# Sparse attention on one core: the compression's first layer in split products, and the query projections spread over more steps

## The chip, the cores and the metric

The kernel runs on one core of a Trainium2 chip. The metric is the device time of one execution in microseconds (us). The core has a matrix engine (PE, with its weight loads shown as PEld), three other compute engines (DVE, ACT, POOL) and a queue that starts transfers (SP). Each engine takes its instructions in the order of the program and waits on semaphores of the others.

## What is computed

The reference is a two-layer decoder trunk on 512 tokens of width 1024: four feed-forward half steps, a gated linear attention with pooling, and, in the second layer, a sparse attention of three branches. The change lies in the sparse attention. Cut to that:

```python
def nsa(h, w_in, cmp_pe, cmpk_w1, cmpk_w2, cmpv_w1, cmpv_w2, w_out):
    q, kc, vc, ks, vs, kw, vw, gates = jnp.split(h @ w_in, cuts, axis=-1)
    ...
    cidx = np.arange(ncmp)[:, None] * 16 + np.arange(32)[None]     # 31 windows of 32 tokens
    def compress(z, w1, w2):
        zb = z[:, cidx] + cmp_pe[None, None, :, None, :]
        zb = zb.transpose(0, 1, 3, 2, 4).reshape(B, ncmp, G, 32 * 64)
        return jax.nn.gelu(zb @ w1) @ w2                           # 2048 -> 256 -> 64
    k_cmp, v_cmp = compress(kc, cmpk_w1, cmpk_w2), compress(vc, cmpv_w1, cmpv_w2)
    # per block of queries: softmax over k_cmp, over the selected keys ks, over the window kw;
    # the three results are gated, added, and projected by w_out
```

There are 16 query heads in 2 key groups, so zb has 62 rows (31 windows by 2 groups) for the keys and 62 for the values.

## The kernel before

**Splitting.** Almost every product is made of float32 values that are split into a high part (float32r, written by ACT) and a low part (the rest, written by DVE or POOL), and takes three one-pass products: hi by hi, lo by hi, hi by lo (`mm3`, L342 to L344). A weight comes by DMA as a raw tile `wr` of 128 x 1024, then `half_hi` (L206, ACT) and `half_lo` (L218, DVE; in the attention loop L216, POOL) write `wh` and `wl` in two halves of 512 columns. The first layer of the compression is the exception: its weights (units "w1", eight of them, four for keys and four for values) are not split, and `hidden` (L1356) multiplies plain float32 tiles, `Z` by `wr`.

**The stream of weights.** `W.next` hands out the next unit. `W.pump(n)` issues loads and conversions for units up to n ahead (n is 2 where nothing is said), at the place in the program where it stands. There are three raw tiles and three pairs `wh`, `wl`; a load waits until the raw tile three units earlier is done with, a conversion until the products with the pair three conversions earlier are done.

**The order at the start of the sparse attention** (`mixer1`; PE, DVE and ACT follow it as written):

1. project kc; finish the norm; pump (splits the unit ks)
2. project vc; get `rstd`; `relay("k")` (L1300, 4 DVE operations), `windows("k")` (L1307, 2 DVE operations that make Z); `negb`; pump (unit w1 of keys, part 0: nothing to split); `relay("v")`, `windows("v")`
3. `keys(0)`: project ks; pump(3) (reaches w1 part 1 and kw); `kf`, `k2`, four ACT copies `kA`, two DVE operations `kB`
4. `hidden(0, "k", 0)`: parts 0 and 1, each followed by a pump
5. `keys(1)`: project kw, then as in 3
6. `hidden(0, "k", 2)`: parts 2 and 3
7. project query block 0 (unit qq0); pump; `gelu(0)` (L1363 to L1370); `qevac(0, ...)` (L1239, L1246, L1250, L1254)
8. `hidden(1, "v", 0)`, whose first pump splits the unit vsw 0; `values` part 0 with it; `hidden(1, "v", 2)`; `values` parts 1 and 2, and `values_out` (L1272 to L1278)

**The attention loop** goes over steps t; head pair m has twelve steps, in each of which scores (L1467), row maxima, exponentials, transposes (L1514), splits of the transposed weights (L1525, L1534) and products with values (L1546, L1548) of different heads stand beside each other. `QP` says in which of the twelve steps how many of the 24 products (`qproj`, L1232) of the next head pair's query projection are issued, `QEV` in which steps the parts of its evacuation (`qevac`) stand, and `FILL` puts the splits of finished outputs (`osplit`) and early products of the output projection (`oproj`) into the last steps. The query projection has one bank of PSUM, tile X.

Of the kernel before, what the change touches and what calls it, by code (L numbers as in the profile page):

```python
# [6 lines left out]
F32 = mybir.dt.float32  # L7
F32R = mybir.dt.float32r
BF = mybir.dt.bfloat16
U32 = mybir.dt.uint32  # L10
AF = mybir.ActivationFunctionType
# [18 lines left out]
def half_step():  # L30

    ev = [(t, 2 * q + e) for q in range(PLAIN) for t in "gu" for e in range(2)]
    m0, end = 2 * PLAIN, len(PARTS) - 1
    d = [("d", p, i, 0, PARTS[p]) for p in range(end) for i in DORD]
    for m in range(m0, 22):
        x, y = (d.pop(0) if d and m > m0 else None for _ in range(2))
        if m == m0:
            ev += [(n, m) for n in (1, 2, 5, 6)]  # L40
        else:
            ev += [e for e in ((1, m), (2, m), (7, m - 1), (5, m), x, (6, m), (3, m - 1), (4, m - 1), y) if e]
    ev += [(7, 21), (4, 21), (3, 21)] + [("d", end, i, 0, 4) for i in DORD[:2]]
    return ev + [("d", end, i, 4 * (n < 2), PARTS[end]) for n, i in enumerate(DORD)]


def unit_shapes():
    out = []

    def ffn(j):  # L50
        for e in half_step():
            if e[0] in ("g", "u"):
                out.append(((e[0], j, e[1]), 1024, True))
            elif e[0] == 1:
                q, t = divmod(e[1], 2)
                for f in (2 * q, 2 * q + 1):
                    out.append((("gu"[t], j, f), 1024, True))
            elif e[0] == "d" and e[3] == 0:
                out.append((("d", j, e[1], e[2]), PARTS[e[1]] * 128, True))

    ffn(0)
    out.append((("gr",), 128, True))
    for nm in ("k0", "k1", "q0", "q1"):
        out.append(((nm,), 1024, True))
    for i in range(4):
        out.append((("v", i), 1024, True))
    for i in (3, 2, 1, 0):
        out.append((("p", i), 1024, True))
    for i in range(4):
        out.append((("gg", i), 1024, True))  # L70
    for d in range(KB):
        out.append((("ao", d), 1024, True))
    ffn(1)
    ffn(2)
    for nm in ("kc", "vc"):
        out.append(((nm,), 1024, True))
    out.append((("ks",), 1024, True))
    for nx in (("w1", 0, 0), ("w1", 0, 1), ("kw",), ("w1", 0, 2), ("w1", 0, 3), ("qq", 0), ("w1", 1, 0), ("w1", 1, 1),
               ("vsw", 0), ("w1", 1, 2), ("w1", 1, 3), ("vsw", 1), ("vsw", 2)):
        n = 304 * (VPART[nx[1] + 1] - VPART[nx[1]]) if nx[0] == "vsw" else 1024  # L80
        out.append((nx, n, nx[0] != "w1"))
    for m in range(1, KB):
        out.append((("qq", m), 1024, True))
    for d in range(KB):
        out.append((("co", d), 1024, True))
    ffn(3)
    return out
# [9 lines left out]
def _build(ctx, tc, nc, a, stages):  # L97
# [10 lines left out]
    V, S, P, TE = nc.vector, nc.scalar, nc.gpsimd, nc.tensor  # L108
    f32 = lambda ap: ap.bitcast(F32)
# [3 lines left out]
    for k in range(KB):  # L113
        t = res.tile([128, T], F32, name=f"h{k}")
# [7 lines left out]
    zero = cst.tile([128, 64], F32, name="zero")  # L122
# [6 lines left out]


    units = [u for u in unit_shapes()]

    def used(key):
# [104 lines left out]
    W = Stream()  # L238
# [945 lines left out]
    def mixer1(nm, nxt):  # L1184
        with ExitStack() as c:
# [24 lines left out]
            o = [op_.tile([128, T], F32, name=f"o{m}") for m in range(KB)]  # L1210
# [70 lines left out]
            with ExitStack() as c2:  # L1281
                s2 = c2.enter_context(pool("m1t", 1, reuse_waits="tile"))
# [3 lines left out]
                R, Z = {}, {}  # L1286
# [4 lines left out]
                def pn():  # L1291
                    return ps.tile([128, T], F32, name="pn", bufs=2)
# [8 lines left out]
                    R[nmx] = r  # L1301

                def windows(nmx):
                    z = s2.tile([128, 1024], F32, name="Z" + nmx)[:, 0:992].rearrange(
                        "p (a b c) -> p a b c", a=16, b=2)
                    for s in range(2):
                        V.tensor_add(z[:, 8 * s:8 * s + 8],  # L1307
                                     R[nmx][:, :, s:s + 31, :].rearrange("p g n r -> p r g n"),
                                     vec[:, C_PE + 8 * s:C_PE + 8 * s + 8][:, :, None, None]
                                     .to_broadcast([128, 8, 2, 31]))  # L1310
                    Z[nmx] = z

                pn0 = pn()
                pkc = pj()
# [8 lines left out]
                V.tensor_scalar(rhalf, rcol, 0.5, None, op0=OP.mult)  # L1323
                relay("k", pkc)
                windows("k")
                V.tensor_copy(negb, neg)
                W.pump()
                relay("v", pvc)
                windows("v")

                def keys(br, key):
# [16 lines left out]
                def hidden(wi, nmx, i0):  # L1348
                    if i0 == 0:
                        hbank[wi] = pn()  # L1350
                    ph = hbank[wi]
                    for i in range(i0, i0 + 2):
                        _, _, raw = W.next("w1", wi, i)
                        for q in range(4):
                            kt = 4 * i + q
                            TE.matmul(ph[0:62, 0:256], Z[nmx][:, kt].rearrange("p a b -> p (a b)"),  # L1356
                                      raw[:, q * 256:(q + 1) * 256], start=kt == 0, stop=kt == 15)
                        W.pump()

                def gelu(wi):  # L1360
                    ph = hbank[wi]
                    x = s2.tile([62, 256], F32, name="gx", bufs=2)
                    V.tensor_copy(x, ph[0:62, 0:256])  # L1363
                    u = aq.tile([62, 256], F32, name="gu", bufs=2)
                    V.tensor_mul(u, x, x)
                    V.tensor_scalar(u, u, 0.044715, 1.0, op0=OP.mult, op1=OP.add)
                    V.tensor_mul(u, u, x)
                    S.activation(u, u, AF.Tanh, scale=0.7978845608028654)
                    V.tensor_scalar(u, u, 1.0, 0.5, op0=OP.add, op1=OP.mult)
                    V.tensor_mul(u, u, x)  # L1370
                    hid.append(u)

                keys(0, "ks")
                hidden(0, "k", 0)
                keys(1, "kw")
                qload(0)
                hidden(0, "k", 2)
                bank = pj()
                for k in range(KB):
# [224 lines left out]
            NU = len(U)  # L1604
            W.pool_lo = True
            at_t = lambda t: (U[t // 3], t % 3) if 0 <= t < 3 * NU else None
            QEV = ({8: 0, 9: 1, 10: 2, 12: 3, 14: 4, 16: 6, 19: 5}, {11: 0, 12: 1, 13: 2, 14: 3, 16: 4, 17: 6, 18: 5})
            QP = {}
            for m, k, ws in ((1, 3, (3, 3, 2, 3, 4, 1, 4, 4)), (2, 0, (3, 3, 3, 4, 3, 3, 3, 2)),
                             (3, -2, (2, 2, 3, 2, 4, 2, 3, 2, 2, 2))):  # L1610
                QP[m] = {k + i: (sum(ws[:i]), sum(ws[:i + 1])) for i in range(len(ws))}
            CMP = ({5: 0, 6: 1, 8: 2, 11: 3, 12: 4}, {5: 0, 6: 1, 9: 2, 10: 3, 12: 4})
            CMPW = {1: (-2, 0), 3: (0, 1), 5: (1, 3)}
# [15 lines left out]

            begun = {0: 7, 1: 5}  # L1630
            FILL = {}
            for m, t in enumerate((84, 84, 87, 89, 90, 92, 97)):
                where = (xp, ("xh", 8), ("xl", 8)) if m < 4 else (aq, ("qA", 3), ("qB", 4))
                FILL.setdefault(t, []).append((osplit, m, P if m < 6 else V, *where))
            for n, t in enumerate((93, 95, 98, 98)):
                FILL.setdefault(t, []).append((W.half, n % 2 * 512))
            for n, t in enumerate((88, 90, 90, 94, 94, 96, 98, 103, 104, 104, 104, 106)):
                d, k = divmod(n, begun[0])
                FILL.setdefault(t, []).append((oproj, d, k, k + 1))
            for t in range(-3, 3 * NU + 11):  # L1640
# [14 lines left out]
                if at_t(t - 1):  # L1655
                    u, x = at_t(t - 1)
# [6 lines left out]
                if at_t(t - 8):  # L1663
                    u, x = at_t(t - 8)
                    pv(u, x)
                for lag in range(3):
                    if at_t(t - 8 - lag):
                        u, x = at_t(t - 8 - lag)
                        if x == 2 and u[2] == 1:
                            out_head(u[0], u[1], lag)  # L1670
                for d in (0, 1):
                    if 1 <= m1 - d < KB and k2 + 12 * d in QEV[m1 - d == 1]:
                        qevac(m1 - d, QEV[m1 - d == 1][k2 + 12 * d])
                m, k3 = divmod(t, 12)
# [51 lines left out]
    for i, s in enumerate(stages):  # L1726
        if s == "fin":
            with ExitStack() as c:
# [4 lines left out]
                p = bank[7]  # L1733
# [26 lines left out]
                for n in range(8):  # L1760
                    t = ob_.tile([128, T], F32, name=f"ot{n}")
# [11 lines left out]
        if s[0] == "f":  # L1773
            ffn(int(s[1]), nm, nxt, sp, i == 0)
        elif s == "m0":
            mixer0(nm, nxt)
        else:
            mixer1(nm, nxt)
        nm = nxt
        if last:  # L1780
            out = a["out"].rearrange("(k a) d -> k (a d)", k=KB).rearrange("k (p t) -> k p t", t=T)
# [5 lines left out]
def layout(i):  # L1787
# [8 lines left out]
    wout, cout = A("a_w_out")[0], A("c_w_out")[0]  # L1796
    w1 = [A("c_cmpk_w1")[0], A("c_cmpv_w1")[0]]
    for key, n, sp in unit_shapes():
        t = key[0]
        if t in ("g", "u"):  # L1800
# [98 lines left out]
```

## Time and profile before

| what | us |
|---|---|
| time, median of 3 runs | 1883.29 (1882.26 to 1884.13) |
| the profiled execution's own time | 1881.94 |
| its span, first to last instruction | 1880.1 |
| PE busy | 1853.3 (99%) |
| PEld busy | 1651.5 (88%) |
| DVE busy | 1474.6 (78%) |
| ACT busy | 969.7 (52%) |
| POOL busy | 636.3 (34%) |

Between the span and the execution's own time lie 1.8 us outside the instructions. A share of busy time is a mean over stages. A matmul's duration holds the time in which its results drain, so successive ones overlap: what a row of matmuls costs is read from the distance between their starts.

### The profile page before, as it was taken

To read this page: it belongs to the slowest core of one execution; us is meant where nothing else is said; L and a number is where in the kernel's file an instruction comes from. 1 tells how busy PE (TensorE), PEld (TensorE's weight loads), DVE (VectorE), ACT (ScalarE), POOL (GpSimd) and SP (SyncE) were. 2 spreads that over 40 slices of the span, in tenths; PEclk is the share of its full clock that TensorE was granted. 3 is DMA by queue.
4 is the path that set the end of the run, shared out by engine and by line. 5 is a ranking of instruction groups with operands and counts; after the bars stand their busy time and mean duration, and the time that the engine had idled before them with its cause. 6 is when DMAs were issued, how large, how long until landed. Compare 5 with 4: busy or idle time off the path is not lost. (4 is left out here: it accounts for less than half of the span.)

```text
span 1880.1 us, 30824 instructions
## 1 busy us (share of the span) xinstructions
PE 1853.3 (99%) x11564; PEld 1651.5 (88%) x11564; DVE 1474.6 (78%) x2414; ACT 969.7 (52%) x1971; POOL 636.3 (34%) x555
## 2 busy tenths in 40 slices
PE   7999999999999999999999999999999999999998
PEld 5999999878889999998899999878887889999997
DVE  7888877656679888876988787756888678978884
ACT  6544445443455454444544444536888645444443
POOL 1433332203123333322343333113556424333321
PEclk9999999999999999999999999999999999999999
DMA  5233322221232323222322223232000132222221
GB/s 190 85 102 102 102 102 96 77 96 57 79 135 79 112 91 116 99 84 89 119 102 101 102 101 105 89 121 74 30 30 27 55 132 85 102 101 102 102 96 62
DMA packets 62007, 175.12 MB, mean 93 GB/s; under 512 B 7520, under 2 KB 9744, under 8 KB 61856
## 3 DMA queue, kind: packets, MB, share of 16 engines
q1 hardware_dynamic: 60544, 171.68, 26.7%
q8 instruction: 91, 1.49, 0.3%
q10 hardware_dynamic: 576, 1.05, 0.2%
q0 software_dynamic: 736, 0.41, 0.1%
q14 instruction: 60, 0.49, 0.1%
HBM read 171.01 MB, written 2.10 MB: 92 GB/s over the span
## 5 line engine op out<-in xcount | busy, mean ns | idle before, releaser
L541 DVE TENSOR_TENSOR wl<-wr,wh 128x512 fp32r<-128x512 f32 (+1 forms) x312 | 280.3, 920 | 6.7 <-ACT wh L538 3.2
L538 ACT ACTIVATE wh<-wr 128x512 fp32r<-128x512 f32 (+1 forms) x312 | 179.3, 603 | 202.6 <-PE pd L343 172.8
L342 PE MATMUL pd<-ahi,wh 128*128 128x512 f32 x704 | 275.6, 391 | 0.0
L343 PE MATMUL pd<-alo,wh 128*128 128x512 f32 x704 | 275.5, 391 | 0.0
L344 PE MATMUL pd<-ahi,wl 128*128 128x512 f32 x704 | 273.9, 389 | 0.0
L677 DVE TENSOR_TENSOR sl<-T,sh 128x512 fp32r<-128x512 f32 x288 | 245.4, 861 | 25.0 <-ACT sh L676 22.4
L676 ACT ACTIVATE sh<-T 128x512 fp32r<-128x512 f32 x288 | 180.5, 627 | 57.9 <-PE z L713 55.0
L711 PE MATMUL xy<-xh,sh 128*128 128x256 f32 x576 | 163.4, 284 | 2.2 <-ACT U L729 2.2
L712 PE MATMUL z<-xs,sh 128*128 128x256 f32 x576 | 163.0, 283 | 0.0
L711 PE MATMUL z<-xs,sh 128*128 128x256 f32 x576 | 163.0, 283 | 0.0
L713 PE MATMUL xy<-xh,wl 128*128 128x256 f32 x576 | 163.0, 283 | 0.0
L713 PE MATMUL z<-xs,sl 128*128 128x256 f32 x576 | 163.0, 283 | 0.0
L712 PE MATMUL xy<-xl,sh 128*128 128x256 f32 x576 | 163.0, 283 | 0.0
L712 PE MATMUL xy<-xl,wh 128*128 128x256 f32 x576 | 163.0, 283 | 0.0
L713 PE MATMUL xy<-xh,sl 128*128 128x256 f32 x576 | 163.0, 283 | 0.0
L657 POOL TENSOR_TENSOR T<-wg,wr 128x512 f32<-128x512 f32 x36 | 49.9, 1387 | 333.6 <-DMA wg<-in_wts_dram 276.4
L711 PE MATMUL xy<-xh,wh 128*128 128x256 f32 x576 | 162.6, 282 | 0.0
L344 PEld LDWEIGHTS pd<-ahi,wl 128*128 128x128 f32 x704 | 132.2, 188 | 28.5
L769 DVE SCALAR_TENSOR_TENSOR h<-pd,h 128x512 f32<-128x512 f32 (+1 forms) x161 | 109.8, 683 | 59.0 <-PE pd L344 58.1
L342 PEld LDWEIGHTS pd<-ahi,wh 128*128 128x128 f32 x704 | 132.7, 188 | 24.1
L343 PEld LDWEIGHTS pd<-alo,wh 128*128 128x128 f32 x704 | 132.7, 189 | 22.5
L657 POOL TENSOR_TENSOR T<-wg 128x512 f32<-128x512 f32 x72 | 108.2, 1503 | 54.6 <-DVE sl L677 54.6
(422 smaller groups left out, 5175.5 us busy)
## 6 DMA issues: line engine op xcount, KB each, us to landing
wr<-in_wts_dram SPq DMA_DIRECT2D x119, 512.0 KB, 3.5
wg<-in_wts_dram SPq DMA_DIRECT2D x72, 512.0 KB, 3.5
wr<-in_wts_dram SPq DMA_DIRECT2D x128, 256.0 KB, 3.7
wf<-in_wts_dram SPq DMA_DIRECT2D x36, 512.0 KB, 4.1
wr<-in_wts_dram SPq DMA_DIRECT2D x32, 384.0 KB, 3.2
h<-in_xt_dram SPq DMA_DIRECT2D x8, 256.0 KB, 4.8
cb<-in_cbias_dram SPq DMA_DIRECT2D x8, 128.0 KB, 3.5
out_dram<-ot ACTq DMA_DIRECT2D x4, 256.0 KB, 2.9
```

The lines of the kernel that those rows point to most:

```text
L342: TE.matmul(out, wh, xh, start=first, stop=False)
L343: TE.matmul(out, wh, xl, start=False, stop=False)
L344: TE.matmul(out, wl, xh, start=False, stop=last)
L538: S.activation(w.t[0][:, c], b.t[:, c], AF.Copy)
L541: V.tensor_sub(w.t[1][:, c], b.t[:, c], f32(w.t[0][:, c]))
L657: return lambda: P.tensor_tensor(o.t, x(), y(), op=op)
L676: s = act(T, lambda: S.activation(w.t[0], src(), AF.Copy), (dep,), (w, b))
L677: return w, dve(T, lambda: V.tensor_sub(w.t[1], src(), f32(w.t[0])), (s,), (w, b), True)
L711: TE.matmul(out, wh, xh[:, q], start=start, stop=False, skip_group_check=True)
L712: TE.matmul(out, wh, xl[:, q], start=False, stop=False, skip_group_check=True)
L713: TE.matmul(out, wl, xh[:, q], start=False, stop=k == 3, skip_group_check=True)
L769: return lambda: V.scalar_tensor_tensor(h[d][:, c], b.t[:, c], 0.5, h[d][:, c], op0=OP.mult, op1=OP.add)
```

## The change

The units w1 are split like all other weights, so each of the eight now has two ACT and two DVE operations of 512 columns. `windows` makes, in two halves, Z as a scratch value (in tiles of the outputs `o`, not yet in use), its high part (ACT) and its low part (DVE), side by side in one tile of 126 columns: 62 high, 2 zeros, 62 low. `hidden` multiplies this tile as the stationary side by the high and by the low weights, 256 columns each: 16 one-pass products for two units, where there were 8 float32 products. `gelu` adds the two stacked halves of the result (one ACT copy more). In the loop, QP spreads the projections of query blocks 3 to 7 over steps -1 to 9 of twelve (before: -2 to 7), that of block 2 over 0 to 9 (before: 0 to 7); QEV moves the evacuations of blocks 2 to 7 by one or two steps; FILL moves six `osplit` and six `oproj` entries forward by one to four steps.

```diff
@@ -78,7 +78,7 @@
         n = 304 * (VPART[nx[1] + 1] - VPART[nx[1]]) if nx[0] == "vsw" else 1024
-        out.append((nx, n, nx[0] != "w1"))
+        out.append((nx, n, True))
@@ -1301,14 +1301,19 @@
                 def windows(nmx):
-                    z = s2.tile([128, 1024], F32, name="Z" + nmx)[:, 0:992].rearrange(
-                        "p (a b c) -> p a b c", a=16, b=2)
+
+                    zz = s2.tile([128, 16, 128], F32R, name="Z" + nmx)
+                    S.activation(zz[:, :, 62:64], zero[:, None, 0:2].to_broadcast([128, 16, 2]), AF.Copy)
                     for s in range(2):
-                        V.tensor_add(z[:, 8 * s:8 * s + 8],
+                        z, a8 = o[2 * len(Z) + s][:, 0:496], slice(8 * s, 8 * s + 8)
+                        V.tensor_add(z.rearrange("p (a b c) -> p a b c", a=8, b=2),
                                      R[nmx][:, :, s:s + 31, :].rearrange("p g n r -> p r g n"),
                                      vec[:, C_PE + 8 * s:C_PE + 8 * s + 8][:, :, None, None]
                                      .to_broadcast([128, 8, 2, 31]))
-                    Z[nmx] = z
+                        z = z.rearrange("p (a b) -> p a b", a=8)
+                        S.activation(zz[:, a8, 0:62], z, AF.Copy)
+                        V.tensor_sub(zz[:, a8, 64:126], z, f32(zz[:, a8, 0:62]))
+                    Z[nmx] = zz
@@ -1350,18 +1355,20 @@
-                        _, _, raw = W.next("w1", wi, i)
+                        whl = W.next("w1", wi, i)[0:2]
                         for q in range(4):
                             kt = 4 * i + q
-                            TE.matmul(ph[0:62, 0:256], Z[nmx][:, kt].rearrange("p a b -> p (a b)"),
-                                      raw[:, q * 256:(q + 1) * 256], start=kt == 0, stop=kt == 15)
+                            for n, w in enumerate(whl):
+                                TE.matmul(ph[0:126, 0:256], Z[nmx][:, kt, 0:126], w[:, q * 256:(q + 1) * 256],
+                                          start=kt + n == 0, stop=kt + n == 16)
                         W.pump()
                 def gelu(wi):
                     x = s2.tile([62, 256], F32, name="gx", bufs=2)
-                    V.tensor_copy(x, ph[0:62, 0:256])
                     u = aq.tile([62, 256], F32, name="gu", bufs=2)
+                    S.activation(u, ph[64:126, 0:256], AF.Copy)
+                    V.tensor_add(x, ph[0:62, 0:256], u)
@@ -1604,10 +1611,10 @@
-            QEV = ({8: 0, 9: 1, 10: 2, 12: 3, 14: 4, 16: 6, 19: 5}, {11: 0, 12: 1, 13: 2, 14: 3, 16: 4, 17: 6, 18: 5})
+            QEV = ({10: 0, 11: 1, 12: 2, 13: 3, 16: 4, 18: 6, 20: 5}, {11: 0, 12: 1, 13: 2, 14: 3, 16: 4, 17: 6, 18: 5})
             QP = {}
-            for m, k, ws in ((1, 3, (3, 3, 2, 3, 4, 1, 4, 4)), (2, 0, (3, 3, 3, 4, 3, 3, 3, 2)),
-                             (3, -2, (2, 2, 3, 2, 4, 2, 3, 2, 2, 2))):
+            for m, k, ws in ((1, 3, (3, 3, 2, 3, 4, 1, 4, 4)), (2, 0, (2, 3, 2, 3, 2, 2, 3, 2, 3, 2)),
+                             (3, -1, (2, 2, 2, 2, 3, 2, 2, 2, 3, 2, 2))):
@@ -1629,12 +1636,12 @@
-            for m, t in enumerate((84, 84, 87, 89, 90, 92, 97)):
+            for m, t in enumerate((80, 81, 83, 85, 87, 90, 97)):
                 where = (xp, ("xh", 8), ("xl", 8)) if m < 4 else (aq, ("qA", 3), ("qB", 4))
                 FILL.setdefault(t, []).append((osplit, m, P if m < 6 else V, *where))
-            for n, t in enumerate((88, 90, 90, 94, 94, 96, 98, 103, 104, 104, 104, 106)):
+            for n, t in enumerate((84, 86, 88, 90, 92, 94, 98, 103, 104, 104, 104, 106)):
```

## Rows read from the trace of the kernel before

**Rows 1.** Page, part 1: busy us (share of the span) and instructions.

```profile
PE 1853.3 (99%) x11564; PEld 1651.5 (88%) x11564; DVE 1474.6 (78%) x2414; ACT 969.7 (52%) x1971; POOL 636.3 (34%) x555
```

**Rows 2.** Waits of PE: what it waited for, us, times, longest us.

```profile
PE xy L342 <- ACT wh L538: 4.6, 1, 4.6
PE T L1514 <- DVE PTl L1534: 2.6, 6, 0.8
PE X L1232 <- DVE VS L1278: 0.9, 1, 0.9
```

**Rows 3.** Stretches: length, then PE, PEld, DVE, ACT, POOL busy, PEclk, DMA.

```profile
24.80:28.00 3.20, 2.87 (x7) 1.80 (x6) 3.20 (x6) 2.51 (x6) 0.00 (x0) 0.50 0.22 35
...
1329.00:1437.00 108.00, 108.00 (x712) 91.80 (x711) 90.67 (x218) 88.23 (x259) 64.12 (x101) 1.00 0.08 26
1437.00:1479.00 42.00, 38.33 (x243) 30.59 (x242) 34.17 (x82) 36.43 (x104) 30.10 (x41) 1.00 0.08 27
```

**Rows 4.** Timeline of PE around the first float32 products: start, us, engine, line.

```profile
1242.03 0.39 PE L344 MATMUL pj<-xh,wl 128*128 128x512 f32 x1
1242.35 3.66 PE L1356 MATMUL pn<-wr,Zk 128*62 128x256 f32 x16
1245.94 0.50 PE L342 MATMUL pj<-xh,wh 128*128 128x512 f32 x1
1246.28 0.39 PE L343 MATMUL pj<-xl,wh 128*128 128x512 f32 x1
```

**Rows 5.** Timeline of PE in a feed-forward stage: one-pass products of 256 columns.

```profile
1000.11 0.28 PE L713 MATMUL z<-xs,sl 128*128 128x256 f32 x1
1000.23 0.28 PE L711 MATMUL z<-xs,sh 128*128 128x256 f32 x1
```

**Rows 6.** Timeline of DVE from the first relay to the low half of vsw.

```profile
1237.64 1.73 DVE L1300 TENSOR_TENSOR Rk<-pj,rstd 64x256 f32<-64x256 f32 x4 [1.82 <-ACT rstd L338]
1239.41 2.13 DVE L1307 TENSOR_TENSOR Zk<-Rk,vec 128x496 f32<-128x496 f32 x2
...
1245.37 1.28 DVE L218 TENSOR_TENSOR wl<-wr,wh 128x512 fp32r<-128x512 f32 x2
1246.68 0.69 DVE L1336 TENSOR_TENSOR kf<-pj,rstd 128x512 f32<-128x512 f32 x1
...
1249.39 0.68 DVE L1343 TENSOR_TENSOR kB<-k,kA 64x512 fp32r<-64x512 f32 x1 [0.57 <-ACT kA L1341]
...
1256.74 0.42 DVE L1363 COPY gx<-pn 62x256 f32<-62x256 f32 x1
...
1260.99 0.69 DVE L1239 SCALAR_TENSOR_TENSOR qf<-pj,rstd 128x512 f32<-128x512 f32 x1 [1.38 <-PE pj L1232]
1262.37 0.69 DVE L1250 TENSOR_TENSOR qA<-qf,qA 64x512 fp32r<-64x512 f32 x1 [0.70 <-ACT qA L1246]
1263.55 1.18 DVE L218 TENSOR_TENSOR wl<-wr,wh 128x512 fp32r<-128x512 f32 x2 [0.49 <-ACT wh L206]
1272.04 1.18 DVE L218 TENSOR_TENSOR wl<-wr,wh 128x512 fp32r<-128x512 f32 x2 [7.30 <-ACT wh L206]
```

**Rows 7.** Timeline of ACT in the same stretch.

```profile
1247.41 0.63 ACT L1341 ACTIVATE kA<-kf 64x512 fp32r<-64x512 f32 x1 [7.29 <-DVE kf L1336]
...
1251.34 1.15 ACT L206 ACTIVATE wh<-wr 128x512 fp32r<-128x512 f32 x2 [1.33 <-DMA wr<-in_wts_dram]
```

**Rows 8.** Timeline of PE: the first product of `values`.

```profile
1264.47 0.41 PE L342 MATMUL pj<-wh,xh 128*128 128x304 f32 x1
```

**Rows 9.** Timeline of PE near the start: a long wait, then matmuls.

```profile
24.46 0.60 PE L342 MATMUL xy<-xh,wh 128*128 128x512 f32 x1 [4.60 <-ACT wh L538]
...
26.83 0.63 PE L343 MATMUL xy<-xl,wh 128*128 128x512 f32 x1
27.26 0.63 PE L344 MATMUL xy<-xh,wl 128*128 128x512 f32 x1
```

**Rows 10.** Page, part 6: loads, count, KB each, us from issue to landing.

```profile
wr<-in_wts_dram SPq DMA_DIRECT2D x119, 512.0 KB, 3.5
```

## The prediction

> **What bounds the kernel.** I read the page first, then PE's waits, then the stretches, then the timelines of PE, DVE and ACT around the two places that change. PE is busy for 99% of the span [rows 1], and its waits are few [rows 2]: a change helps if it takes work off PE, and harms if it makes PE wait. The distance between starts tells what PE work costs: in the first stretch of float32 products PE goes from one ordinary product at 1242.03 over sixteen records to the next at 1245.94 and its successor at 1246.28 [rows 4]. In the attention loop from 1329 to 1437 us PE is busy for 108.00 of 108.00 us, so nothing but PE work sets that pace; from 1437 to 1479, where the last head pair has no projection beside it any more, PE idles for 42.00 - 38.33 = 3.67 us [rows 3]. The reader should see one thing more: just before the float32 products DVE runs without a break, from the first relay at 1237.64 to kB [rows 6], so what is added to DVE's queue there comes out late.
>
> **Products, on PE.** Ordinary 512-column products start 0.227 us apart (1242.03 would have been followed at 1242.26; the 1246.28 product stands for 1246.05). So one stretch costs 1246.05 - 1242.26 = 3.79 us [rows 4]; there are four, 15.2 us. After, a stretch has 16 one-pass products of 256 columns. No row shows one with 126 stationary columns; the nearest are those of the feed-forward stage, 0.12 us apart with a new weight load each [rows 5]: 1.92 us. PE saves 1.87 us a stretch, 7.5 us in all. If nothing else happened this would be the gain.
>
> A rule of the Trainium skill speaks against it: *TensorE: Matmul & The Clock Gate*, Part 3, says that a weight load overlaps running matmuls only where the row group differs, and its section on LDWEIGHTS prices a load at columns / 1.2 ns, here an estimate of 105 ns. By it a stretch would cost 16 x (0.107 + 0.105) = 3.4 us, an estimate, and nearly nothing would be saved. The row with loads of the same shape shows 0.12 us from start to start, so the trace does not agree, and the sum goes by the row.
>
> **Conversions, on ACT and DVE.** The eight w1 units now need two ACT and two DVE operations each: 1.15 us a unit on ACT [rows 7], 1.28 on DVE [rows 6]. `windows` was two DVE additions, 2.13 us together. Now each half is an addition (1.07), an ACT copy of 496 columns, and a DVE subtraction that waits for that copy. No row shows these two on this layout; the nearest are a conversion's halves, 0.60 on ACT and 0.68 on DVE; I take these and 0.05 for each handover: 2.45 a half, 4.9 for a `windows`. The addition with its awkward strides (1.07) is the bound above, 0.4 more for each of the eight operations, +3.1; below, the layout could save no more than the columns missing from 512 and the handovers, -0.8.
>
> What matters is where these stand. DVE's queue, laid out in program order from the first relay:
> - relay k 1.73, from 1237.64 to 1239.4; windows k 4.9, to 1244.3; negb 0.2 and the lows of w1 part 0, 1.28, to 1245.8 (the first half at 1245.1).
> - relay v 1.73, windows v 4.9: to 1252.4. Only then, because the pump of `keys(0)` stands behind them, w1 part 1 (to 1253.7) and kw (to 1255.0). On ACT the highs of part 1 stand behind the copies of windows v just so.
> - kf to kB of the first keys took 1250.07 - 1246.68 = 3.4 before [rows 6]: to 1258.4. Then parts 2 and 3, 2.56 and some 0.4 since their highs stand behind the four kA copies on ACT (0.63 each [rows 7]): to 1261.3; qq0 to 1262.6; the second keys to 1266.0.
> - values' parts 0 and 1, 3.0: to 1269.0; gelu, 1256.74 to 1259.61, 2.9 (its new ACT copy lies beside these lows): to 1271.9; qf, qA: 1260.99 to 1263.06, 2.1: to 1274.0; 0.5 for ACT; vsw part 0: 1274.5, first half at 1275.2.
>
> **Loads** follow the same queue: a raw w1 tile is now freed by DVE's low instead of PE's product. Part 3 and qq0 can load from 1253.7 and 1255.0, and land 3.5 later [rows 10], at 1257.2 and 1258.5, before ACT has time for them at 1258.0 and 1260: no new wait but a few tenths.
>
> **PE** beside it: ks ends at 1242.26, `hidden` waits until 1245.1 (2.9), gets through part 0 by 1246.1, **waits for part 1 until 1253.0** (6.9), starts kw at 1254.3 and ends it at 1259.8 (24 x 0.227), does parts 2 and 3 by 1261.7, starts qq0 at about 1261.8, ends it at 1267.3, does two values' parts by 1269.2 and **waits for vsw until 1275.2** (6.0). Before, values began at 1264.47 [rows 8]: 10.7 us later. From there the work is the same but for one stretch that is 1.87 shorter; DVE's further lows fit into its idle 7.30 us [rows 6]. So values end 8.9 us later. Before, X then waited 0.9 us for the VS operations of DVE [rows 2], which after are less far behind; I take back 0.4: **+8.5 us**. The saving on PE is inside this: it is eaten because PE arrives earlier at weights that come later. If DVE had been idle there, the conversions would have cost nothing.
>
> **The clock.** At 24.46 PE came back from a wait of 4.60 us [rows 9], and in the stretch from 24.80 to 28.00 the granted clock was 0.50, the lower level of 1.2 GHz [rows 3]; products there start 0.43 us apart instead of 0.227 [rows 9]. Two waits above are longer than 4.6. After the first of them DVE, not PE, is the later one: a kw projection that loses half of 3.3 us ends at 1261.5, before DVE asks for it at 1262.6, so it hides. After the second the values follow and carry it to the end: half of about 3.3 us, 1.7, with bounds of 0 (the drop falls into the wait) and 3.4 (two such stretches). I take **+1.7**.
>
> **The loop.** Until the last head pair the spread moves PE work between steps and none away, and PE has no idle there: nothing to win. qf now frees the bank X one step ahead of the next projection instead of two, and the last qA part stands one step ahead of its scores; two more products (0.46 us) in each of two steps that had none give DVE that time. In the last steps the later projections and the earlier `osplit` and `oproj` can fill at most the 3.67 us of PE idle and the drain of some ten waits (0.39 - 0.227 = 0.16 each; the six longest stand in [rows 2]), 5.3; and each earlier `osplit` puts 0.63 us of ACT [rows 7] and a subtraction of POOL into steps in which PE waits for DVE's PTl already. I take **-1**, between -4 and +1.
>
> **Sum:** 8.5 + 1.7 - 1 = +9.2 us, on the profiled execution's 1881.94: 1891.1; that execution lies 1.35 under the median, so the median becomes **1892.5**. Bounds: 8.5 - 0.8 - 4 = +3.7 with no clock loss, 1887; 8.5 + 3.1 + 3.4 + 1 = +16, 1899.
>
> **Rivals.**
> 1. *The conversions hide and PE's saving stands* (faster): decided by whether w1 part 1 and vsw reach PE in time. For it: DVE idles 7.30 us in one piece later in the stage [rows 6]. Against: that idle time lies behind the places that wait. It would give -7.5 - 1, 1874.8. 7%.
> 2. *The waits are there, but short, and the tail gains all it can* (no change): halves of `windows` run overlapped, no clock loss, -4 in the tail: +1 to +4, about 1886. 10%.
> 3. *The loop gets worse too*: X waits for qf at each of five starts and scores for qA at six, 0.3 us each, 3.3 on top: 1896 or a little more. 7%.
> 4. *The products save nothing* (the change does not do what it says: more than one pass, or weight loads that don't hide): a stretch costs 3.8 as before. Against: the 0.12 of [rows 5]. Three of the four stretches end in a wait for DVE anyway; the one among the values then costs 1.9 more, 1894.4. 2%. The Trainium skill's rule on weight loads, above, would make it so.
>
> **How the numbers follow.** The forecast has 74%. The measurement tells 0.2%, 3.8 us, from no change: between 1879.5 and 1887.1 counts as the same. Faster: rival 1 and a little of 2, 8%. Same: most of rival 2, 9%. Slower: 83%. The range goes from 1886, rival 2's middle, to 1898, short of the corner where all bad bounds meet: it leaves out rival 1, half of rival 2 and that corner.
>
> **What will show it.** Right: PE rows with a wait of 6 to 7 us before the second w1 unit and of about 6 before values, ended by DVE's or ACT's halves of the weights; a granted clock of 0.5 after them; `hidden` at 0.12 us from start to start; the loop's middle still without idle; values beginning near 1275. Wrong: values that begin before 1266, a loop whose middle has PE idle, or a tail that loses its 3.67 us wholly.

## The result, and the profile after

| | us |
|---|---|
| before, median | 1883.50 (1882.26 to 1884.13) |
| after, median of 4 runs | 1905.74 (1905.21 to 1906.03) |
| ratio | 1.0119, 95% interval 1.0107 to 1.0131 |
| predicted | 1892.5, range 1886 to 1898 |

The change costs 22.2 us. The direction was predicted; the size was missed by 13, outside the range.

The page of after, part 1 (columns as in [rows 1]): PE has the same number of instructions and is busy for 5.5 us longer.

```profile
PE 1858.8 (98%) x11564; PEld 1658.3 (87%) x11564; DVE 1487.1 (78%) x2434; ACT 982.5 (52%) x1995; POOL 634.0 (33%) x555
```

PE's waits after (columns as in [rows 2]). The compression's products have moved to L1362, the scores from L1467 to L1474, their exponentials from L1493 to L1500.

```profile
PE pn L1362 <- ACT wh L206: 7.4, 2, 5.7
...
PE pj L342 <- ACT wh L206: 4.5, 1, 4.5
PE S L1474 <- ACT P L1500: 4.0, 6, 0.7
...
PE T L1521 <- DVE PTl L1541: 3.0, 4, 1.4
PE S L1474 <- DVE qA L1250: 2.7, 6, 0.5
```

The first two lines are the forecast: w1's units (5.7 of the 7.4 us is the second one) and the first product of `values` wait for weights. The third and fifth, scores that wait for exponentials and for qA, are in none of [rows 2] (before has two waits for exponentials, 0.6 us in all, in its last steps); they come six times each, once per head pair.

Timeline of PE after, for [rows 4] and [rows 8]. The whole trace lies 0.96 us later than before's here (1242.99 for 1242.03). The code up to here is the same in both: the shift is 0.4 us where [rows 9] begin and 1.0 us from 30 us on, where the granted clock was at 0.50 for 6.8 us from the end of that wait on, and for 3.4 in before.

```profile
1242.99 0.39 PE L344 MATMUL pj<-xh,wl 128*128 128x512 f32 x1
1245.06 0.38 PE L1362 MATMUL pn<-wh,Zk 128*126 128x256 f32 x1 [1.68 <-ACT wh L206]
...
1252.90 0.58 PE L1362 MATMUL pn<-wh,Zk 128*126 128x256 f32 x1 [5.68 <-ACT wh L206]
...
1262.42 0.28 PE L1362 MATMUL pn<-wh,Zk 128*126 128x256 f32 x1
1262.54 0.28 PE L1362 MATMUL pn<-wl,Zk 128*126 128x256 f32 x1
...
1276.33 0.62 PE L342 MATMUL pj<-wh,xh 128*128 128x304 f32 x1 [4.51 <-ACT wh L206]
```

The values begin at 1276.33 for 1264.47, 10.9 us later once the 0.96 is taken off.

Timeline of DVE after, for [rows 6]: two halves of one `windows`, a low that comes late, the second `windows`, and the conversions behind it.

```profile
1240.38 1.11 DVE L1309 TENSOR_TENSOR o<-Rk,vec 128x496 f32<-128x496 f32 x1
1242.17 0.68 DVE L1315 TENSOR_TENSOR Zk<-o,Zk 128x496 fp32r<-128x496 f32 x1 [0.69 <-ACT Zk L1314]
1242.77 1.07 DVE L1309 TENSOR_TENSOR o<-Rk,vec 128x496 f32<-128x496 f32 x1
1244.52 0.68 DVE L1315 TENSOR_TENSOR Zk<-o,Zk 128x496 fp32r<-128x496 f32 x1 [0.68 <-ACT Zk L1314]
...
1252.95 2.49 DVE L218 TENSOR_TENSOR wl<-wr,wh 128x512 fp32r<-128x512 f32 x4
...
1263.10 1.29 DVE L218 TENSOR_TENSOR wl<-wr,wh 128x512 fp32r<-128x512 f32 x2 [1.12 <-ACT wh L206]
...
1276.31 3.58 DVE L218 TENSOR_TENSOR wl<-wr,wh 128x512 fp32r<-128x512 f32 x6 [0.49 <-ACT wh L206]
```

Stretches after (columns as in [rows 3]): two of the start stage, the middle of the loop, and one in the last steps.

```profile
1248.60:1258.60 10.00, 5.49 (x16) 4.52 (x17) 7.97 (x12) 5.64 (x10) 0.00 (x0) 0.50 0.37 112
1275.90:1282.50 6.60, 6.07 (x22) 5.74 (x23) 3.58 (x6) 2.88 (x6) 0.00 (x0) 0.50 0.55 161
1341.00:1449.00 108.00, 102.67 (x651) 83.92 (x650) 84.47 (x202) 82.15 (x242) 55.38 (x93) 1.00 0.08 26
...
1470.40:1473.80 3.40, 3.40 (x15) 3.25 (x14) 2.42 (x8) 2.25 (x7) 1.81 (x3) 0.50 0.00 0
```

The third line is the surprise: PE was busy for 108.00 of 108.00 us there in [rows 3], and now idles for 5.33. From the starts of the scores: the second step of attention begins 10.9 us later (shift taken off), the 78 steps from there take 163.14 us for 152.78, **10.4 more**, and the next 16 steps 33.53 for 31.90, 1.6 more. 10.9 + 10.4 + 1.6 + 0.96 (the shift) is 23.9 of the 24.1 us between the two profiled executions (1906.03 and 1881.94): nearly half lies where the prediction had -1.

What happens in the loop stands in one stretch of it: rows of DVE, ACT and PE around the start of a head pair.

```profile
1388.73 0.67 DVE L1250 TENSOR_TENSOR qA<-qf,qA 64x512 fp32r<-64x512 f32 x1
...
1389.73 0.62 DVE L1495 TENSOR_REDUCE st<-S 128x1 f32<-128x128 f32 x2
...
1390.44 0.37 ACT L1500 ACTIVATE P<-S,st 128x128 f32<-128x128 f32 x1 [1.65 <-POOL P L1510]
...
1391.25 0.62 ACT L1254 ACTIVATE qB<-qA 64x512 fp32r<-64x512 f32 x1
...
1392.29 0.57 ACT L1500 ACTIVATE P<-S,st 128x384 f32<-128x384 f32 x1
...
1393.02 0.50 PE L1474 MATMUL S<-kA,qA 128*128 128x256 f32 x2 [0.68 <-ACT P L1500]
```

The low of qA (moved to this step) stands in front of the row maxima; ACT idles 1.65 us until they are done at 1390.35. (The row names POOL as releaser. But all sixteen waits of this kind between 1300 and 1440 us end 0.09 to 0.10 us after the row maxima, and 0.03 to 0.15 after POOL's last; and what POOL does there waits itself for two small DVE operations that stand between qA's low and the row maxima.) Next on ACT stands the copy of qB, moved here too, in front of the exponentials of 384 columns. These free the bank that PE's scores want: PE waits until 1393.02. Which of these moves matters is the question of the experiments below.

### The profile page after: what moved, and what is told of

It reads as the page before. It is cut to its first block, busy times and chain, and to the rows that moved or that the text cites. A ratio compares the mean times of both kernels' runs of the same rounds, so it can differ in the third digit from the quotient of the medians.

```text
span 1904.2 us, 30877 instructions
## 1 busy us (share of the span) xinstructions
PE 1858.8 (98%) x11564; PEld 1658.3 (87%) x11564; DVE 1487.1 (78%) x2434; ACT 982.5 (52%) x1995; POOL 634.0 (33%) x555
## 4 chain that ended last, share of the span: by engine, by line
PE 86%; DVE 6%; ACT 5%; issue 2%; DMA 1%; POOL 0%; SPq 0%; POOLq 0%; ACTq 0%; DVEq 0%
PE xy L711 9%; PE xy L713 9%; PE xy L712 9%; PE pd L342 8%; PE pd L343 8%; PE pd L344 8%; PE z L711 4%; PE z L712 4%; PE z L713 4%; PE pj L342 3%; PE pj L343 3%; PE pj L344 3%; ACT P L1500 1%; PE xy L344 1%; PE z L342 1%
## 5 line engine op out<-in xcount | busy, mean ns | idle before, releaser
L342 PEld LDWEIGHTS pd<-ahi,wh 128*128 128x128 f32 x704 | 132.7, 189 | 24.1
```

The source lines that it names most:

```text
L342: TE.matmul(out, wh, xh, start=first, stop=False)
```

## The experiments

All are taken against the kernel before, 1883.2 to 1883.6 in these runs. "Period" is the time from one head pair to the next (12 steps), read from the starts of the scores: 23.57 us before, 25.51 after, in the middle of the loop.

### The parts alone

**e1**, the compression alone: after, with the loop's tables of before.

```diff
-            QEV = ({10: 0, 11: 1, 12: 2, 13: 3, 16: 4, 18: 6, 20: 5}, ...
+            QEV = ({8: 0, 9: 1, 10: 2, 12: 3, 14: 4, 16: 6, 19: 5}, ...
   (QP and both lists of FILL likewise)
```

> The changed kernel with QP, QEV and FILL as before: only the compression's first layer, the conversions and gelu are changed. Theory A (the two parts add up; the loop's new waits come from its own placing): the start costs what the trace of the changed kernel shows there, attention step 1 about 11 us later, the loop's period is 23.6 us again, and the time is 1883.5 + 11 = 1894 to 1895. Theory B (the loop's waits are inherited: engines enter the loop later and in another order, and never regain it): the loop keeps its period of 25.5 us and the time stays near 1905.

1894.79, ratio 1.0063 (1.0048 to 1.0078): **+11.2**. The period is 23.57 again. PE's waits keep those of the start and lose those of the scores:

```profile
PE pn L1362 <- ACT wh L206: 6.7, 2, 5.0
...
PE pj L342 <- ACT wh L206: 4.5, 1, 4.5
```

**e2**, the loop alone: before, with QEV, QP and FILL of after.

> The kernel before with the new QP, QEV and FILL alone: compression as before. Theory A: period 25.5 us instead of 23.6, with PE waiting in each for ACT's exponentials (0.7 us), DVE's qA (0.5 us) and a little for qf; +10 to +12 us, 1894 to 1895. Theory B: period 23.6 us, the time within 2 us of before.

1895.71, ratio 1.0068 (1.0053 to 1.0083): **+12.1**. 11.2 + 12.1 = 23.3 against the 22.2 of the whole change: the two halves add, to about one us (theory A). The loop's waits are its own, and not handed down from the late start (theory B).

**e3**, FILL alone.

```diff
-            for m, t in enumerate((84, 84, 87, 89, 90, 92, 97)):
+            for m, t in enumerate((80, 81, 83, 85, 87, 90, 97)):
   (and the list of oproj steps likewise)
```

> The kernel before with the new FILL alone (earlier splits of finished outputs and earlier first products of the output projection). If the earlier filler fills PE's idle time in the last steps, as the prediction's -1 had it: 1880 to 1883. If the earlier ACT and POOL work of the splits delays the exponentials and transposes there, and PE's waits draw the clock down as in the changed kernel: 1885 to 1887.

1883.95, ratio 1.0004 (0.9994 to 1.0013): nothing. Stretches of its last steps, the first of them that of [rows 3]:

```profile
1437.00:1479.00 42.00, 38.55 (x241) 31.30 (x240) 33.27 (x82) 35.35 (x103) 29.49 (x42) 0.96 0.08 26
1447.70:1450.90 3.20, 3.20 (x14) 2.63 (x14) 1.82 (x4) 3.16 (x10) 2.65 (x4) 0.50 0.00 0
```

PE idles for 3.45 instead of 3.67 us, and the clock falls for 3.2 us, which it did nowhere in that stretch before. The earlier filling wins next to no idle time back. The fall is not FILL's doing: e15 below has the same FILL and the same waits there (its longest 0.96 us, as in e3), and no fall; e13, with the old FILL, has one.

**e4**, QP and QEV alone.

> The kernel before with the new QP and QEV, FILL as before. Theory A with all of the loop's loss in QP and QEV: period 25.5 us, +10 us, 1893 to 1894, that is nearly the whole of the loop-only run. If FILL is what costs: within 2 us of before.

1895.08, ratio 1.0064 (1.0049 to 1.0079): **+11.5**, all of the loop's loss. Period 25.51. PE's waits:

```profile
PE S L1467 <- ACT P L1493: 4.0, 6, 0.7
PE S L1467 <- DVE qA L1250: 3.5, 6, 1.2
```

### The start stage

**e5**, e1 with w1's part 1 converted ahead of the windows of v.

```diff
-                W.pump()
+                W.pump(3)
                 relay("v", pvc)
```

> As e1 (compression changed, loop old; 1894.8), but the four conversions of w1 part 1 are queued ahead of the v windows, not behind them. Theory Q (what sets when the values begin is DVE's whole queue up to the vsw weights): the wait before part 1 shrinks from 5.0 us to about 1.5, but the wait only moves behind it, because the same DVE work still stands ahead of kw, the keys and vsw; 1894 to 1895, at most 1 less if the clock is not lowered. Rival R (the first long wait is itself what the start loses): 5 us less, near 1890.

1893.51, ratio 1.0053 (1.0038 to 1.0068): -1.3. The wait before part 1 went from 5.0 to 1.7 us and came back as one of 4.7 before kw. Theory Q holds: the long wait was where the queue's length shows, not its cause.

**e6**, e1 with both additions of `windows` ahead of both subtractions.

```diff
-                        V.tensor_sub(zz[:, a8, 64:126], z, f32(zz[:, a8, 0:62]))
+                        zs.append((z, a8))
+                    for z, a8 in zs:
+                        V.tensor_sub(zz[:, a8, 64:126], z, f32(zz[:, a8, 0:62]))
```

> As e1, but windows makes both halves' additions before both halves' subtractions, so that DVE does not stand still during ACT's copy of the first half. Theory Q: two windows, each with about 1.4 us of DVE standing still removed, 2.8 us less than e1: about 1892. Rival (DVE's queue is not what sets the values' start): the same as e1, 1894.8.

1890.75, ratio 1.0042 (1.0028 to 1.0056): -4.0 for an expected -2.8. Four times 0.69 us in which DVE stood still for ACT (two of them in the rows of after above) were worth the 2.8, and the clock the rest, it seems: in the three stretches of 20 us from 1240 the granted clock was 0.67, 0.93 and 0.90 in e1, and 0.83, 0.83 and 1.00 here.

**e7**, e6 with w1's lows on POOL, and the windows of v and the first value unit moved.

```diff
-            elif self.pool_lo:
+            elif self.pool_lo or key[0] == "w1":
...
-                relay("v", pvc)
-                windows("v")
   (these two now behind the last W.pump() ahead of the first gelu,
    then hidden(1, "v", 0), the four qevac(0, e), gelu(0))
```

> As e6, and further: the subtractions for the lows of w1 go to POOL, the relay and windows of v stand behind the conversions of qq's part 0, and the first value unit with the vsw conversions stands ahead of the first gelu. All of the change's operations are still made. Theory Q: with nothing of the new work ahead of the weights that PE waits for, most of the 11 us of e1 comes back: 1884 to 1887, no wait of PE over about 3 us in the start, no fall of the granted clock there. Rival (the start loses by the products of the stacked windows themselves, or by ACT's share of the work, which stays): above 1890.

1889.49, ratio 1.0031 (1.0020 to 1.0042): only half of the 11.2 came back, so theory Q's 1884 to 1887 was missed. PE waited 2.9 us for the lows on POOL, where a half takes 1.28 us in the attention loop of before (0.68 on DVE at the start), and 4.3 us for the second `windows`. Rows of DVE's second `windows` in e7, and of POOL beside it:

```profile
1264.26 2.95 DVE L1310 TENSOR_TENSOR o<-Rv,vec 128x496 f32<-128x496 f32 x2
1267.14 3.37 DVE L1318 TENSOR_TENSOR Zv<-o,Zv 128x496 fp32r<-128x496 f32 x2
1263.16 6.80 POOL L216 TENSOR_TENSOR wl<-wr,wh 128x512 fp32r<-128x512 f32 x4 [5.18 <-ACT wh L206]
```

**e12**, e7's order with nothing on POOL.

```diff
-            elif self.pool_lo or key[0] == "w1":
+            elif self.pool_lo:
```

> As e7 (1889.5), same order of the queues, but the lows of w1 are subtracted on DVE again, none on POOL. Theory N (in e7 the start loses by POOL: its 1.46 us for a half against DVE's 0.68 makes PE wait in the first stretch, and DVE's windows of v ran slower beside it): PE's first stretch ends 3 us earlier, values begin earlier, 1886 to 1888. Rival (DVE's sum of work is the bound, and gets 5 us longer): 1891 or more.

1885.60, ratio 1.0013 (1.0003 to 1.0022): theory N, and 0.4 below its range. DVE makes sixteen more subtractions (ten us at 0.64) and is done earlier. The same two rows of DVE, with POOL idle:

```profile
1263.16 1.99 DVE L1310 TENSOR_TENSOR o<-Rv,vec 128x496 f32<-128x496 f32 x2
1265.07 1.45 DVE L1318 TENSOR_TENSOR Zv<-o,Zv 128x496 fp32r<-128x496 f32 x2
```

2.88 us less for the same four operations, and PE's wait for them is the only long one that is left in the stage:

```profile
PE pn L1363 <- DVE Zv L1318: 6.0, 1, 6.0
```

1885.60 is 2.4 above before's 1883.24 in the same runs. So of the compression's 11.2 us, 8.8 were the order in which DVE and ACT take their work, and 2.4 remain while everything that the change adds is still computed. The wait of 6.0 us that is left, with a fall of the granted clock around its end (0.87 on average from 1263 to 1290 us), stands against the 7.5 that the products save; no run tried to take it away.

### The loop

**e8**, e4 with the last low of qA one step earlier.

```diff
-            QEV = ({10: 0, 11: 1, 12: 2, 13: 3, 16: 4, 18: 6, 20: 5}, ...
+            QEV = ({10: 0, 11: 1, 12: 2, 13: 3, 16: 4, 18: 6, 19: 5}, ...
```

> As e4 (projections spread, compression and fill old; 1895.1), but the last low part of a query projection is evacuated one step earlier. Theory L1 (the loop's two waits are separate, each priced by its own place): the wait of the scores for qA goes, 0.63 us in each of six periods, 3.8 less: about 1891.3; the wait for the exponentials stays. Theory L2 (DVE and ACT have as much to do as before, so the time only moves to another wait): about 1895.

1893.59, ratio 1.0052 (1.0037 to 1.0067): -1.5, between the theories. PE's waits from 1280 to 1490 us:

```profile
PE S L1467 <- ACT P L1493: 4.1, 6, 0.7
...
PE X L1232 <- DVE qf L1239: 1.9, 5, 0.4
```

The wait for qA is gone; but PE, earlier now, waits longer at the next projection for the bank that qf frees (0.4 us in all in after). Part of the gain only moved.

**e9**, before, with the even spread of blocks 3 to 7 but begun one step earlier, so that QEV stays.

```diff
-                             (3, -2, (2, 2, 3, 2, 4, 2, 3, 2, 2, 2))):
+                             (3, -3, (2, 2, 2, 2, 3, 2, 2, 2, 3, 2, 2))):
```

> The kernel before, with the projections of the third and later head pairs spread over eleven steps of two or three products as the change does, but beginning one step earlier than before (at -3) and ending where they ended, so that all evacuations keep their old steps. Theory E (the loop loses by the steps into which the evacuations were moved): period 23.6 us as before, 1883.5, at most 1 more. Theory F (it loses by the even spread, which leaves some step with too little PE work ahead of its scores): period near 25.5, about 1894.

1883.11, ratio 0.9999 (0.9990 to 1.0009).

**e10**, e4 with the ten-step counts of before, begun one step later.

```diff
-                             (3, -1, (2, 2, 2, 2, 3, 2, 2, 2, 3, 2, 2))):
+                             (3, -1, (2, 2, 3, 2, 4, 2, 3, 2, 2, 2))):
```

> As e4 (1895.1), with the evacuations in the steps of the change, but the projections of the third and later head pairs over ten steps with the product counts of before, begun one step later. Theory E: the loss stays, 1894 to 1896, with the scores waiting for the exponentials and for qA in every period. Theory F: the loss goes, about 1884 to 1886.

1894.97, ratio 1.0064 (1.0049 to 1.0079). The stretch of [rows 3], first in e9, then in e10:

```profile
1329.00:1437.00 108.00, 108.00 (x709) 91.41 (x707) 90.42 (x217) 89.14 (x265) 64.05 (x103) 1.00 0.08 26
```

```profile
1329.00:1437.00 108.00, 102.39 (x652) 84.59 (x651) 84.24 (x202) 82.10 (x241) 55.48 (x92) 1.00 0.08 26
```

Theory E: the even spread costs nothing (108.00 of 108.00), and the old counts, when they come a step later with the late evacuations, lose as much as the change does. It is the later steps that cost, not the evenness. e10 moves projections and evacuations together; the evacuations alone, qf left out, follow in e13 and e14.

**e11**, e8 with four products instead of two in the step ahead of the wait for exponentials.

```diff
-                             (3, -1, (2, 2, 2, 2, 3, 2, 2, 2, 3, 2, 2))):
+                             (3, -1, (2, 2, 2, 4, 2, 2, 2, 2, 2, 2, 2))):
```

> As e8 (1893.6), but four products instead of two in the step before the one where the scores wait for the exponentials, taken from two other steps. Theory G (that wait exists because PE reaches the scores early; work in front of it fills it): the wait of 0.66 us shrinks to 0.2 or less in each of six periods, 2.5 to 4 less than e8: 1889.5 to 1891. Theory H (DVE and ACT are late in that stretch by their own queues, and PE then waits one or two steps later): the time stays at about 1893.5.

1890.52, ratio 1.0040 (1.0025 to 1.0055): -3.1, theory G. The wait shrank from 4.1 to 1.9 us in six periods, and the wait for qf from 1.9 to 0.4 in one.

**e13** and **e14**, before, with the evacuations of one head alone moved.

```diff
-            QEV = ({8: 0, 9: 1, 10: 2, 12: 3, 14: 4, 16: 6, 19: 5}, ...
+            QEV = ({8: 0, 9: 1, 12: 2, 13: 3, 14: 4, 16: 6, 19: 5}, ...     (e13)
+            QEV = ({8: 0, 9: 1, 10: 2, 12: 3, 16: 4, 18: 6, 20: 5}, ...     (e14)
```

> The kernel before, with two operations alone moved: the low of the first head's qA from step 10 to 12 and the copy of its qB from 12 to 13; the division (qf) stays at 8, the projections are those of before. Theory K (these two, in front of the row maxima and the exponentials of the steps before the next head pair, make the scores wait for the exponentials): that wait shows with 0.5 to 0.8 us in each of six periods, the wait for qA does not; 1887 to 1889. Theory M (DVE and ACT have room for them; the loss needs the later division or PE's lighter steps): 1883.5, no such wait.

> The kernel before, with the three operations of the second head alone moved as the change moves them (16, 18 and 20 for 14, 16 and 19). Theory K: the scores of the second head wait for qA's low, which now stands one step ahead of them, about 0.6 us in each of six periods, and nothing waits for the exponentials; 1886.5 to 1888. Theory M: 1883.5.

e13: 1885.72, ratio 1.0011 (1.0002 to 1.0021), +2.3; e14: 1887.52, ratio 1.0022 (1.0013 to 1.0032), +4.1. PE's wait in e14:

```profile
PE S L1467 <- DVE qA L1250: 4.2, 6, 1.3
```

For the second head theory K holds to the figure. For the first it holds at a smaller price. The list of waits shows nothing there, because it leaves out idle times under 0.15 us, and the end of PE's last product covers the rest. The starts show it: PE at the start of a head pair, and ACT just ahead, in before and then in e13:

```profile
1376.13 0.60 PE L1581 MATMUL S<-ident,ce 128*64 128x128 f32 x4
1376.48 0.48 PE L1467 MATMUL S<-kA,qA 128*128 128x256 f32 x2
1375.84 0.23 ACT L1493 ACTIVATION_READ_ACCUMULATOR P<-S,st 128x1 f32 x1
```

```profile
1377.54 0.60 PE L1581 MATMUL S<-ident,ce 128*64 128x128 f32 x4
1378.18 0.51 PE L1467 MATMUL S<-kA,qA 128*128 128x256 f32 x2
1377.93 0.20 ACT L1493 ACTIVATION_READ_ACCUMULATOR P<-S,st 128x1 f32 x1
```

In before ACT is done with the exponentials at 1376.07, 0.41 us ahead of the scores. In e13 it is done at 1378.13 and the scores start 0.05 us later, 0.64 us behind the row above them instead of 0.35: 0.29 us more, which is the whole growth of the period (23.86 for 23.57).

The same reading prices all three waits, by the distance from the start of the product ahead: for exponentials 0.03 us in before, 0.32 in e13, 0.56 in e11, 0.95 in e8 and e4; for qA 0.08 in before, 0.75 or more in e14, 0.72 in e4; for qf 0.26 in before, 0.53 in e4, 0.85 in e8. So the later places alone make the scores wait for the exponentials. Two products fewer ahead of them (0.45 us of PE work) lengthen the wait, and so does something else that e11 has and e13 has not: the later qf, the later projections or the second head's places. e9, with the light step and the old places, has no wait.

2.3 + 4.1 is 6.4 of the loop's 11.5. By these distances e4 loses 0.92 us a head pair to the exponentials, 0.64 to qA and 0.27 to qf, 1.83 of the 1.94 by which its period grows. So most of the other 5 is the longer wait for exponentials (0.92 for e13's 0.29), and the rest qf. qf was not moved alone.

### Both places mended

**e15**: e12's compression, e9's spread, e3's FILL.

> All three parts of the change with both places mended: the compression as in e12, the projections spread over eleven steps with the evacuations in their old places as in e9, and the earlier fill as in e3. If the parts add, as the first four runs had them: 1885.6 + 0 + 0.4, about 1885.5 to 1886.5, near the kernel before. If the earlier fill loses its clock in the tail here without gaining first, 1887.

1885.86, ratio 1.0013 (1.0003 to 1.0022). All three parts of the change are in it, for 2.5 us instead of 22.2: the parts add here too. It isn't faster than the kernel before; nothing run here is.

## Why the prediction missed

**The step that failed is "The loop".** It put the spread, its evacuations and FILL at -1 (between -4 and +1). e4 measures +11.5 for the first two, and FILL, from which most of the -1 was to come, gives nothing (e3). The argument, "no idle there: nothing to win", was right about PE and asked the wrong engine. PE's idle of zero in [rows 3] was a balance: DVE and ACT delivered the row maxima, exponentials and qA just in time. The prediction counted PE's products per step, but not who stands behind each moved evacuation on DVE and ACT. The rows above show them: row maxima behind qA's low, exponentials behind the copy of qB, and scores one step behind the last low.

**Rival 3 named the place and mispriced it.** X waiting for qf and scores for qA are both there (e4, e8, e14). At 0.3 us each and eleven times it gave 3.3. Measured in e4, per head pair: qf 0.27, as priced; qA 0.64, twice the price; and the largest, 0.92 for exponentials, it did not have. With 7% it had no weight in the forecast.

**The start was right, nearly row by row.**
- Products: 0.12 us from start to start with 126 stationary columns (1262.42 to 1262.54), as taken from [rows 5]. Rival 4 falls. The Trainium skill's rule on weight loads (*TensorE: Matmul & The Clock Gate*, Part 3) would have put them at nearly twice that, by the prediction's estimate; the trace of after does not agree either.
- `windows`: 4.9 was taken for one; 1240.38 to 1245.20 is 4.8, each half with the 0.69 us in which DVE stands still for ACT. (Its lower bound, -0.8, comes to -0.6 when its parts are added; nothing hangs on that.)
- PE's waits: 2.9, 6.9 and 6.0 were taken; the trace shows 1.7, 5.7 and 4.5 of idle, each over a us less. The second w1 unit came at 1252.90 (forecast 1253.0, or 1253.96 with the shift: a us early), the values at 1276.33 (forecast 1275.2, or 1276.16), but PE came to them later than forecast. e5, e6 and e12 show that the reason given, DVE's queue in program order, is the cause and not only a picture that fits.
- Clock: +1.7 was taken, with 3.4 as the upper bound. The fall to 0.50 after the wait before the values lasts 6.6 us with 6.07 of PE work, so about 3.0 were lost. The first fall hid behind DVE as argued but for the 1.12 us that DVE idled before 1263.10: qq's first half went to ACT only when kw's last product had gone (its last row starts at 1262.19).
- X's wait for VS [rows 2] was to give back 0.4; it is gone wholly, and the first step gets 1.2 shorter.

10.2 was forecast for the start (8.5 + 1.7), and e1 measures 11.2. That it came so near is in part luck: the clock was taken too small by 1.3 us or more, and what X and the first step give back too small by 0.8. **Rival 1** fell as argued: the conversions don't hide. **Rival 2** fell too: the waits were not short, and the tail gained nothing. With the loop at its measured 11.5 the sum would have been 1881.94 + 1.35 + 10.2 + 11.5 = 1905.0, against 1905.74.

## What to carry over

Zero idle on the bounding engine says that there is nothing to win on it, and nothing at all about what there is to lose: before an evacuation is moved, write down on its own engine's queue what will stand behind it, and how long the bounding engine can go on without that. A change that moves work off PE onto a helper's in-order queue is priced by that queue's order; here the same added work cost 11.2 us in one order and 2.4 in another. A wait of PE that grows where two changes meet (a later operation and a lighter step) is found by doing each alone and both, not by adding them; and a wait too short for the list of waits is found by the distance between starts.

## What was not expected of the hardware

- POOL and DVE took turns. Two additions and two subtractions of `windows` took 2.95 and 3.37 us with POOL's subtractions beside them (e7), 1.99 and 1.45 without (e12); POOL's own halves took 1.70 on average (6.80 for four), and 1.28 in the attention loop of before. The Trainium skill has a sentence that fits: *Trainium Architecture — The Big Picture*, "What this means for kernel authors", says that on the engines' side of SBUF only the port pair shared by DVE and GpSimd contends, as an exclusive lock. The single rows of e7 agree: from 1264.3 us on the two engines' operations end in strict turns, POOL's each 1.07 to 1.13 us after DVE's, DVE's each 0.53 to 0.82 after POOL's. Not all work collides: POOL's first half took 1.29 beside DVE's relays, and those 0.42 to 0.43 each, as in e12.

```profile
1264.42 1.97 POOL L216 TENSOR_TENSOR wl<-wr,wh 128x512 fp32r<-128x512 f32 x1
1265.24 1.97 DVE L1310 TENSOR_TENSOR o<-Rv,vec 128x496 f32<-128x496 f32 x1
```

- The granted clock fell without a wait as long as that of [rows 9]. In the last steps it stood at 0.50 for 3.2 us in e3 and 3.4 in after, where the longest waits of PE are 1.0 and 1.4 us, and not at all in the same steps of before. The same waits need not bring a fall: e15 has those of e3 there, and stayed at 1.00.
- How long a fall lasts is not fixed either. The two in the start of after held for at least 10.0 and 6.6 us, against the 3.2 of [rows 3]; and the fall of [rows 3] itself, in code that no run changes, lasted 3.4 us in six of the seventeen profiles and 6.8 in the other eleven.
